# A change to the feed-forward half of a decoder layer: plain products for one column set of down, earlier residual loads, token sums split by adding transfers, gelu and splits at a later place on ScalarE

## The chip, the cores and the metric

The kernel runs on one core of a Trainium2 chip. The metric is the device time of one execution in microseconds (us). Engines are named as in the profile: PE is TensorE's matmul, PEld its weight load, DVE is VectorE, ACT is ScalarE, POOL is GpSimd, SP is SyncE, which does nothing here but issue DMAs.

## The reference

A decoder layer for 512 tokens of width 2048 in float32: four attention groups, an output projection, a layer norm, a gated feed-forward part, a second layer norm. The change touches the feed-forward part alone.

```python
D_MODEL, SEQ, D_FF, CONV_WIDTH = 2048, 512, 5632, 3

def conv_ffn(x, w_up, conv_w, conv_b, w_down):
    S = x.shape[1]
    u, g = jnp.split(x @ w_up, 2, axis=-1)
    gp = jnp.pad(g, ((0, 0), (CONV_WIDTH - 1, 0), (0, 0)))
    gc = conv_b
    for tap in range(CONV_WIDTH):
        gc = gc + conv_w[tap] * gp[:, tap:tap + S]
    return (jax.nn.gelu(gc) * u) @ w_down
...
        h = layer_norm(DEEPNORM_ALPHA * h + mix, ln1_g[l], ln1_b[l])
        ffn = conv_ffn(h, ffn_w_up[l], ffn_conv_w[l], ffn_conv_b[l], ffn_w_down[l])
        h = layer_norm(DEEPNORM_ALPHA * h + ffn, ln2_g[l], ln2_b[l])
```

## The kernel before

**Numbers.** A float32 operand is held as a high and a low part in a shorter float format (fp32r); a product is three matmuls (`PARTS`: high-high, high-low, low-high). `split_pair` (L898) makes the parts: ACT copies the raw value into the high part (L899), DVE subtracts that from the raw value into the low part (L900).

**Units.** Both large products of the feed-forward part run in units of 84 matmuls of 128x256. A unit is a Strassen-Winograd step: 2x2 blocks, 7 block products (`UP`) for 8, of 12 matmuls each. Its operands are seven weight blocks (three of the blocks as they are, four sums) and seven token blocks (likewise). The part "up" is units 0 to 87: 44 columns of tiles `f`, two units each. The part "down" is units 88 to 129: `CHUNKS` cuts the hidden rows into three chunks of six row pairs `kp` and one of four; within a chunk the column sets `q` (four; three in the last chunk) run one after the other, each of three units of two `kp` (two units in the last chunk). So unit 88 is the first of down, unit 91 the first of its second column set, and units 100, 112 and 124 are the first of chunks 1, 2 and 3. The last quarter of the columns of the last chunk is done plainly at the end (the tail).

**Weights.** `next_unit` (L902) hands out a unit and at that place has the operands of the following one made by `weight_operands` (L909): SP loads two raw tiles `wr` of 512 KB (four buffers, two units); ACT writes the negative of three blocks into `wl` (L925); a DMA in POOL's queue adds the raw blocks to that in place (L926, 768 KB, so `wl` becomes raw minus its rounded value); ACT copies the blocks into `wh` (L928); POOL makes four sums `S` (L934 to L937), which `split_pair` splits into four `ws` pairs. `wh` and `wl` have two buffers each, `ws` six pairs, `S` two tiles. The first two units (f = 0) use plain products and fewer operands.

**Up's end.** After the second unit of an `f`, `up_finish` (L989) adds up the banks, and `gated` (L1003) makes the gate: ACT `c` (L1010), two DVE steps (L1011, L1013), gelu on ACT (L1015), the product with `up` on POOL (L1016). For every second `f`, `set_aside` makes four token sums `ht` on POOL (L1031 to L1036) and SP writes blocks and sums to HBM (`hid`).

**Hidden operands.** `hidden_operands(kp)` (L1071) has SP load the blocks (`hx`) and the sums (`hx` for a chunk's first two `kp`, `hxt` for the others) and splits them by `split_pair`. It is called for kp 0 to 3 in the first unit of the last `f`, for 4 and 5 at unit 88, and for the next chunk's six in the last column set of a chunk, two after each of its units.

**Down's end of a set.** In the last unit of a set, `down_add` (L1117) adds the seven banks to the accumulators `acc`; in chunk 0 the residual rows are loaded into these at that same unit (L1200).

**Order.** Code is written in the order of use; a scheduler places each instruction on its engine's list by a priority that goes with that order, moved by `high_priority` (weights 900 places ahead, hidden splits 10 ahead in chunk 0, 150 behind later). An engine runs its list in order; a DMA starts from the list of the engine that issues it, so a transfer of POOL's queue waits for all that stands before it on POOL.

## Time and profile before

| | us |
|---|---|
| runs | 2329.66, 2337.31, 2339.68 (median 2337.31) |
| profiled execution | 2341.35 |
| its span | 2339.6 |
| PE busy in the span | 2232.7 (95%) |
| DVE, POOL, ACT busy | 1591.7, 1368.4, 1229.5 |
| software DMA queue (POOL's), share of 16 engines | 102.24 MB, 24.6% |
| hardware DMA queue q1 (SP's) | 287.72 MB, 35.6% |

The span is the profiled execution from its first instruction to its last; 1.75 us of that execution lie outside of it. "Busy" is a sum over the span. PEclk is the granted clock of TensorE as a share of full speed (2.4 GHz; the other level is 1.2 GHz). Up runs from about 920 us to 1829.44, down from there to about 2281, the tail and the last layer norm to the end.

### The profile page before, as it was taken

The page shows a single profiled execution, that of the slowest core. Times are in us where ns is not written, and L with a number is a line of the kernel's source. Part 1 is how long each engine was busy: PE and PEld are TensorE (multiplying, and loading weights), DVE is VectorE, ACT ScalarE, POOL GpSimd, SP SyncE. Part 2 cuts the span into 40 slices and gives each one's busy share as a digit, 9 for nine tenths or more (in the row PEclk, how much of TensorE's full clock was granted, in tenths as well). Part 3 has the DMA queues.
Part 4 walks back from the last instruction along what each step waited for, and adds up shares of the span by engine and source line. Part 5 has one row for each costly group of instructions (what it writes and reads, how often), then busy time and mean ns, then how long its engine had stood idle before and what let it go on. Part 6 is the DMA issues. An engine that isn't in the chain of part 4 may idle for free. (4 is left out here: it accounts for less than half of the span.)

```text
span 2339.6 us, 40306 instructions
## 1 busy us (share of the span) xinstructions
PE 2232.7 (95%) x15454; PEld 2083.5 (89%) x15454; DVE 1591.7 (68%) x2204; ACT 1229.5 (53%) x2129; POOL 1368.4 (58%) x1197
## 2 busy tenths in 40 slices
PE   7999999999999998899999999999999899999995
PEld 6788888888888878899999999999999899899994
DVE  7544455456675348687787767777676878677778
ACT  5444453355563135565555555565555666565651
POOL 5212110123234517787887878877777687777874
PEclk9999999999999999999999999999999999999998
DMA  6322223222124363888888777777778888788873
GB/s 228 92 81 73 78 67 106 84 64 62 59 88 149 104 188 94 224 226 227 231 222 238 202 210 207 201 204 197 212 202 227 243 241 233 193 229 216 207 191 115
DMA packets 125362, 392.75 MB, mean 168 GB/s; under 512 B 13632, under 2 KB 23744, under 8 KB 125168
## 3 DMA queue, kind: packets, MB, share of 16 engines
q1 hardware_dynamic: 106304, 287.72, 35.6%
q0 software_dynamic: 18720, 102.24, 24.6%
q8 instruction: 121, 1.98, 0.3%
q14 instruction: 73, 0.60, 0.1%
q10 hardware_dynamic: 144, 0.21, 0.0%
HBM read 354.36 MB, written 35.65 MB: 167 GB/s over the span
## 5 line engine op out<-in xcount | busy, mean ns | idle before, releaser
L900 DVE TENSOR_TENSOR ws<-S,ws 128x512 fp32r<-128x512 f32 x512 | 600.1, 1192 | 244.3 <-ACT ws L899 238.9
L963 PE MATMUL up<-xt,ws 128*128 128x256 f32 x3096 | 386.4, 283 | 0.3 <-DVE ws L900 0.3
L963 PEld LDWEIGHTS up<-xt,ws 128*128 128x128 f32 x3096 | 378.0, 192 | 0.6 <-DVE ws L900 0.6
L899 ACT CAST ws<-S 128x512 fp32r<-128x512 f32 x512 | 307.0, 615 | 114.9 <-POOL S L934 33.5
L100 DVE TENSOR_TENSOR wl<-wr,wh 128x1024 fp32r<-128x1024 f32 x122 | 155.2, 1272 | 213.3 <-ACT wh L99 198.4
L936 POOL TENSOR_TENSOR S<-wr 128x512 f32<-128x512 f32 x128 | 212.0, 1656 | 92.5 <-DVE ws L900 87.3
L342 POOL TENSOR_SCALAR P<-P,r 128x128 f32<-128x128 f32 (+3 forms) x144 | 81.1, 582 | 308.5 <-DVE r L337 166.2
L963 PE MATMUL up<-x,wh 128*128 128x256 f32 x1376 | 258.8, 288 | 0.0
L99 ACT CAST wh<-wr 128x1024 fp32r<-128x1024 f32 x122 | 128.0, 1049 | 233.7 <-PE op L733 78.8
L934 POOL TENSOR_TENSOR S<-wr 128x512 f32<-128x512 f32 x128 | 183.8, 1436 | 108.0 <-issue 45.3
L925 ACT ACTIVATE wl<-wr 128x512 fp32r<-128x512 f32 (+1 forms) x260 | 205.1, 836 | 67.3 <-PE dn L1115 43.5
L928 ACT CAST wh<-wr 128x512 fp32r<-128x512 f32 (+1 forms) x260 | 211.5, 829 | 35.7 <-PE up L963 33.8
L963 PE MATMUL up<-x,wl 128*128 128x256 f32 x688 | 200.8, 292 | 29.5 <-DMA wl<-in_wup_dram 29.3
L963 PEld LDWEIGHTS up<-x,wh 128*128 128x128 f32 x1376 | 220.5, 197 | 0.0
L937 POOL TENSOR_TENSOR S<-wr,S 128x512 f32<-128x512 f32 x128 | 211.8, 1655 | 0.0
L935 POOL TENSOR_TENSOR S<-S,wr 128x512 f32<-128x512 f32 x128 | 198.5, 1551 | 9.7
L1115 PE MATMUL dn<-wh,hx 128*128 128x256 f32 x792 | 157.5, 292 | 13.3 <-DVE acc L1128 8.6
L963 PEld LDWEIGHTS up<-x,wl 128*128 128x128 f32 x688 | 135.8, 197 | 33.7 <-DMA wl<-in_wup_dram 33.7
L1115 PEld LDWEIGHTS dn<-wh,hx 128*128 128x128 f32 x792 | 132.3, 200 | 14.9 <-issue 6.3
L733 PE MATMUL op<-wh,oTs 128*128 128x512 f32 x448 | 140.6, 391 | 0.0
L963 PE MATMUL up<-x,ws 128*128 128x256 f32 x1032 | 137.9, 283 | 0.0
L1015 ACT ACTIVATE c<-c 128x512 f32<-128x512 f32 x44 | 27.8, 632 | 208.0 <-DVE c L1013 208.0
(327 smaller groups left out, 5321.3 us busy)
## 6 DMA issues: line engine op xcount, KB each, us to landing
wr<-in_wup_dram SPq DMA_DIRECT2D x176, 512.0 KB
wl<-in_wup_dram POOLq DMA_DIRECT2D x88, 768.0 KB, 7.5
wr<-in_wm_dram SPq DMA_DIRECT2D x84, 512.0 KB
wr<-in_wdown_dram SPq DMA_DIRECT2D x84, 512.0 KB
wl<-in_wdown_dram POOLq DMA_DIRECT2D x42, 768.0 KB, 7.4
wr<-in_wout_dram SPq DMA_DIRECT2D x32, 512.0 KB
hid<-c SPq DMA_DIRECT2D x44, 256.0 KB
hid<-ht SPq DMA_DIRECT2D x44, 256.0 KB
```

What stands on the lines that cost most here:

```text
L100: nc.vector.tensor_sub(l[:, :cols], raw[:, :cols], h[:, :cols].bitcast(F32))
L733: nc.tensor.matmul(ps, ot[ct][:, a, t * P:(t + 1) * P], w[b][:, c2 * 512:(c2 + 1) * 512], start=(first and (a, b) == (0, 0)), stop=(last a ...
L899: self.nc.scalar.copy(h, raw)
L900: self.nc.vector.tensor_sub(l, raw, h.bitcast(F32))
L925: nc.scalar.mul(l3[:, o], i, -1.0)
L928: nc.scalar.copy(h3[:, o], i)
L934: nc.gpsimd.tensor_add(s12[:, 0], a21, a22)
L935: nc.gpsimd.tensor_sub(s12[:, 1], s12[:, 0], a11)
L936: nc.gpsimd.tensor_sub(s34[:, 0], a11, a21)
L937: nc.gpsimd.tensor_sub(s34[:, 1], a12, s12[:, 1])
L963: self.nc.tensor.matmul(ps, w[iw][i][:, k * P:(k + 1) * P], x[j][ix], start=(opens and k == 0 and (i, j) == (0, 0)), stop=(last and k == 3 ...
L1115: self.nc.tensor.matmul(bk[i][:, a * 256:(a + 1) * 256], x[ix][j][:, a * P:(a + 1) * P], w[iw][p][:, q * 256:(q + 1) * 256], start=first a ...
```

## The change

Four edits, all in the feed-forward part.

1. The first column set of chunk 0 (units 88 to 90) is made of plain products: 48 matmuls of 256 columns and 24 of 512 per unit, on four banks. These units need no weight sums; the low parts of their weights come from DVE (`split_pair`), and not from the adding DMA.
2. In chunk 0 the residual rows are loaded at the first unit of a set and not at its last.
3. `hidden_added`: for the last four `kp` of each chunk (two in the last one), 14 of 22, the low part of the token sums `hxt` is made as that of the weights is: ACT writes the negative, a DMA in POOL's queue adds the 512 KB from HBM, ACT copies the high part in place. These are ACT and POOL instructions of 1024 columns, for two ACT and two DVE instructions of 512 before.
4. `deferred` and `run_deferred`: gelu with what follows it, and all splits of hidden operands, are put behind `mark`, the last ACT copy of the following unit's weights.

The new `plain_products` and `plain_add` are in the diff; the removed body of `hidden_operands` is the one printed above.

```diff
@@ -896,14 +896,24 @@
     def split_pair(self, raw, h, l):
-        self.nc.scalar.copy(h, raw)
+        ins = self.nc.scalar.copy(h, raw)
         self.nc.vector.tensor_sub(l, raw, h.bitcast(F32))
+        return ins
+    def run_deferred(self):
+        with self.tc.issue_after(self.mark.ins):
+            while self.deferred:
+                self.deferred.popleft()()
     def next_unit(self):
         w = self.unit
+        self.w12 = self.w12_next
         self.unit = self.weight_operands(self.units.popleft()) if self.units else None
         self.unit_no += 1
+        self.run_deferred()
         return w
     def weight_operands(self, src):
@@ -913,6 +923,8 @@
         nc = self.nc
         with self.tc.high_priority(offset=900 if self.unit_no > 1 else 200):
+            plain = self.unit_no < 2 or 2 * FT <= self.unit_no < 2 * FT + 3
             raw = [self.pW.tile([P, 2, 512], F32, tag="wr", name="wr", bufs=4) for _ in range(2)]
             for p in range(2):
                 nc.sync.dma_start(raw[p], src[:, 2 * p:2 * p + 2])
@@ -921,14 +933,20 @@
             a22 = raw[1][:, 1]
             h3, l3 = (self.pW.tile([P, 3, 512], F32R, tag=g, name=g, bufs=2)
                       for g in ("wh", "wl"))
-            for o, i in ((slice(0, 1), raw[0][:, 1:2]), (slice(1, 3), raw[1])):
-                nc.scalar.mul(l3[:, o], i, -1.0)
-            nc.gpsimd.dma_start(l3, src[:, 1:4], accum_op=ALU.add)
-            for o, i in ((slice(0, 1), raw[0][:, 1:2]), (slice(1, 3), raw[1])):
-                nc.scalar.copy(h3[:, o], i)
-            if self.unit_no < 2:
+            blocks = ((slice(0, 1), raw[0][:, 1:2]), (slice(1, 3), raw[1]))
+            if self.unit_no < 2 * FT or not plain:
+                for o, i in blocks:
+                    nc.scalar.mul(l3[:, o], i, -1.0)
+                nc.gpsimd.dma_start(l3, src[:, 1:4], accum_op=ALU.add)
+                for o, i in blocks:
+                    nc.scalar.copy(h3[:, o], i)
+            else:
+                for o, i in blocks:
+                    self.split_pair(i, h3[:, o], l3[:, o])
+            if plain:
                 w = [self.tmp("w21", dt=F32R, tag="w") for _ in range(2)]
-                self.split_pair(a21, *w)
+                self.mark = self.split_pair(a21, *w)
+                self.w12_next = h3[:, 1:3], l3[:, 1:3]
                 return [[h3[:, i], l3[:, i]] for i in range(3)] + [w]
             s12, s34 = (self.pP.tile([P, 2, 512], F32, tag="P", name="S") for _ in range(2))
             nc.gpsimd.tensor_add(s12[:, 0], a21, a22)
@@ -939,7 +957,7 @@
             for t in (s12, s34):
                 for i in range(2):
                     ws.append([self.tmp("ws", dt=F32R, tag="w") for _ in range(2)])
-                    self.split_pair(t[:, i], *ws[-1])
+                    self.mark = self.split_pair(t[:, i], *ws[-1])
         return [[h3[:, i], l3[:, i]] for i in range(3)] + ws
@@ -981,7 +999,7 @@
         self.step_aside()
         if (f, n) == (FT - 1, 0):
             for kp in range(4):
-                self.hidden_operands(kp)
+                self.hidden_blocks(kp)
         if n == 1:
             self.up_finish(f, self.bk.pop(f)[0])
@@ -1012,6 +1030,10 @@
                                        op1=ALU.add)
         nc.vector.scalar_tensor_tensor(c[:, 2:], g[:, :510], cw(0), c[:, 2:], op0=ALU.mult,
                                        op1=ALU.add)
+        self.deferred.append(lambda: self.activate(f, c, up))
+    def activate(self, f, c, up):
+        nc = self.nc
         nc.scalar.activation(c, c, AF.Gelu_apprx_tanh)
         (nc.vector if f == 0 else nc.gpsimd).tensor_mul(c, c, up)
         c = c.rearrange("p (a n) -> p a n", a=2)
@@ -1068,45 +1090,96 @@
     SLOTS = 6
-    def hidden_operands(self, kp):
...
+    def hidden_split(self, srcs, tiles):
+        for (h, l), src in zip(tiles, srcs):
             with self.tc.high_priority(offset=10):
...
+                self.nc.sync.dma_start(l.bitcast(F32), src)
+        def split():
+            for h, l in tiles:
+                self.split_pair(l.bitcast(F32), h, l)
+        self.deferred.append(split)
+    def hidden_added(self, src, h, l):
+        nc = self.nc
+        with self.tc.high_priority(offset=10):
+            nc.sync.dma_start(h.bitcast(F32), src)
+        def split():
+            nc.scalar.mul(l, h.bitcast(F32), -1.0)
+            nc.gpsimd.dma_start(l, src, accum_op=ALU.add)
+            nc.scalar.copy(h, h.bitcast(F32))
+        self.deferred.append(split)
+    def hidden_blocks(self, kp):
+        def pair(n):
             if n == 2:
...
+                return [self.tmp("hx", (P, 2, 256), F32R) for _ in range(2)]
+            o = self.tmp("hx", (P, 2, 1, 256), F32R)
+            return o[:, 0], o[:, 1]
+        sizes = (2, 1, 1) if kp < self.SLOTS else (2, 2) if kp >= 18 else (2, 1)
+        tiles = [pair(n) for n in sizes]
+        ops, srcs = [], []
+        for t, n in zip(tiles, sizes):
+            srcs.append(self.hid[kp][:, len(ops):len(ops) + n])
+            ops += [[h[:, k] for h in t] for k in range(n)]
+        self.hidden_split(srcs, tiles)
+        self.ho[kp] = ops
+    def hidden_sums(self, kp):
+        if kp % self.SLOTS >= 2:
+            whole = [self.pT.tile([P, 4, 256], F32R, tag="T", name="hxt") for _ in range(2)]
+            xt = [[x[:, i:i + 2] for x in whole] for i in (0, 2)]
         else:
             xt = [[self.tmp("hx", (P, 2, 256), F32R) for _ in range(2)] for _ in range(2)]
...
+        if kp % self.SLOTS >= 2:
+            self.hidden_added(self.hid[kp][:, 4:8], *whole)
+        else:
+            self.hidden_split([self.hid[kp][:, i:i + 2] for i in (4, 6)], xt)
+        ops = self.ho[kp]
+        self.ho[kp] = (ops[:3] + [[h[:, k] for h in x] for x in xt for k in range(2)] + ops[3:])
+    def plain_products(self, bk, w, u):
+        for k in range(2):
+            ops = self.ho[2 * u + k]
+            cols = slice(k * 256, (k + 1) * 256)
+            for t in range(NT):
+                a = slice(t % 2 * P, t % 2 * P + P)
+                for j, p in self.PARTS:
+                    first = u == 0 and k == 0 and (j, p) == (0, 0)
+                    x1, x2 = (ops[i][j][:, a] for i in ((0, 1), (-1, 2))[t // 2])
+                    for n, iw in enumerate((0, 3)):
+                        self.nc.tensor.matmul(bk[t][:, n * 256:(n + 1) * 256], x1,
+                                              w[iw][p][:, cols], start=first and n == 0,
+                                              stop=False, skip_group_check=True)
+                    self.nc.tensor.matmul(bk[t].rearrange("p (a n) -> p a n", a=2), x2,
+                                          self.w12[p][:, :, cols], start=False,
+                                          stop=u == 2 and k == 1 and (j, p) == (1, 0),
+                                          skip_group_check=True)
+    def plain_add(self, acc, bk):
+        nc = self.nc
+        for t in range(NT):
+            o = acc[t // 2][:, t % 2]
+            if t < 2:
+                nc.vector.tensor_add(o, o, bk[t])
+            else:
+                nc.vector.tensor_add(o[:, :256], o[:, :256], bk[t][:, :256])
+                nc.scalar.copy(o[:, 256:], bk[t][:, 256:])
+        c22 = acc[1][:, :, 256:]
+        for o in (acc[0][:, :, 256:], acc[1][:, :, :256]):
+            nc.gpsimd.tensor_sub(o, o, c22)
     def down_product(self, bk, w, i, q, x, first, last):
         _, _, iw, ix = self.UP[i]
@@ -1181,25 +1254,39 @@
             if n and 2 <= f < 18:
                 self.up_residual(f - 2)
         self.st2 = [self.cst.tile([P, 4, 6], F32, name=f"st2_{t}") for t in range(NT)]
-        self.due = deque((4, 5))
+        self.due = deque()
         acc = []
         token = lambda t, q: acc[q][t // 2][:, t % 2]
         for c, k0, nk in self.CHUNKS:
             sets = self.column_sets(c)
             for q in sets:
-                bk = [self.bank("g" if i < 3 else "a", "dn") for i in range(7)]
+                plain = (c, q) == (0, 0)
+                bk = [self.bank("g" if i < 3 else "a", "dn") for i in range(4 if plain else 7)]
                 nu = nk // 2
                 for u in range(nu):
                     w = self.next_unit()
                     self.step_aside()
-                    if c == 0 and u == nu - 1:
+                    if c == 0 and u == 0:
                         acc.append([self.pT.tile([P, 2, 512], F32, tag="T", name="acc")
                                     for _ in range(2)])
                         for t in range(NT):
                             cols = 512 if t < 2 else 256
                             nc.sync.dma_start(token(t, q)[:, :cols], self.res[t][q][:, :cols])
                     while self.due:
-                        self.hidden_operands(self.due.popleft())
+                        kp = self.due.popleft()
+                        self.hidden_blocks(kp)
+                        self.hidden_sums(kp)
+                    if plain:
+                        if u == 0:
+                            for kp in (4, 5):
+                                self.hidden_blocks(kp)
+                        for kp in (2 * u, 2 * u + 1):
+                            self.hidden_sums(kp)
+                        self.plain_products(bk, w, u)
+                        if u == nu - 1:
+                            self.plain_add(acc[q], bk)
+                        continue
                     for i in range(7):
                         for k in range(2):
                             self.down_product(bk, w, i, k, self.ho[k0 + 2 * u + k],
```

Where instructions stand. The first place is ACT in up, before: `c_13278` is the gate of f = 18, `wh_13410` and `wl_13411` are weights of unit 40 (f = 20), the `ws` are the weight sums of unit 39.

```order
L1010 ACTIVATE c_13278<-g_13268,prm_83 128x512
L1015 ACTIVATE c_13278<-c_13278 128x512
L928 CAST wh_13410<-wr_13406 128x512
L925 ACTIVATE wl_13411<-wr_13406 128x512
L925 ACTIVATE wl_13411<-wr_13407 128x1024
L899 CAST ws_13313<-S_13300 128x512
L928 CAST wh_13410<-wr_13407 128x1024
L899 CAST ws_13317<-S_13300 128x512
```

After, the same instructions:

```order
L1028 ACTIVATE c_13278<-g_13268,prm_83 128x512
L942 CAST wh_13410<-wr_13406 128x512
L939 ACTIVATE wl_13411<-wr_13406 128x512
L939 ACTIVATE wl_13411<-wr_13407 128x1024
L899 CAST ws_13311<-S_13298 128x512
L942 CAST wh_13410<-wr_13407 128x1024
L899 CAST ws_13315<-S_13298 128x512
L1037 ACTIVATE c_13278<-c_13278 128x512
```

Gelu stands six places later, behind the weights; so it does for 40 of the 44 `f`. POOL in up, before (`c_14056` is the gate of f = 21, `wl_14194` a weight of unit 46):

```order
L935 TENSOR_TENSOR S_14200<-S_14200,wr_14189 128x512
L1016 TENSOR_TENSOR c_14056<-c_14056,up_14053 128x512
L1032 TENSOR_TENSOR ht_14184<-c_14056,ht_14184 128x256
L1035 TENSOR_TENSOR ht_14185<-c_14056,c_13799 128x256
L1036 TENSOR_TENSOR ht_14185<-c_14056,ht_14184 128x256
L926 DMA wl_14194<-in_wup_dram 128x1536
```

And after:

```order
L953 TENSOR_TENSOR S_14200<-S_14200,wr_14189 128x512
L940 DMA wl_14194<-in_wup_dram 128x1536
L1038 TENSOR_TENSOR c_14056<-c_14056,up_14053 128x512
L954 TENSOR_TENSOR S_14201<-wr_14189 128x512
L955 TENSOR_TENSOR S_14201<-wr_14190,S_14200 128x512
L1054 TENSOR_TENSOR ht_14184<-c_14056,ht_14184 128x256
```

The DMA that makes `wl` is issued ahead of the product that needs gelu, and no longer behind it and three token sums.

The second place is ACT at the start of chunk 1. Before, `hxt_21371` are token sums of kp 8, `ws_21201` and `ws_21344` weight sums of units 99 and 100, and `wl_21510` belongs to unit 101.

```order
L899 CAST ws_21201<-S_21184 128x512
L899 CAST hx_21383<-hx_21384 128x512
L899 CAST ws_21344<-S_21338 128x512
L899 CAST hx_21386<-hx_21386 128x256
L899 CAST ws_21348<-S_21338 128x512
L899 CAST hxt_21371<-hxt_21372 128x512 x2
L1138 COPY acc_21361<-dn_21048 128x2x256
L925 ACTIVATE wl_21510<-wr_21505 128x512
```

After, `hxt_21286` and `hxt_21285` are the low and the high part of kp 8's sums, `ws_21430` is the last weight sum of unit 101, and `wh_21552` and `ws_21565` belong to unit 102.

```order
L899 CAST ws_21430<-S_21413 128x512
L942 CAST wh_21552<-wr_21549 128x1024
L899 CAST ws_21565<-S_21559 128x512
L899 CAST hx_21280<-hx_21281 128x512
L899 CAST ws_21569<-S_21559 128x512
L899 CAST hx_21282<-hx_21282 128x256
L1113 ACTIVATE hxt_21286<-hxt_21285 128x1024
L899 CAST hx_21288<-hx_21289 128x512
L1115 CAST hxt_21285<-hxt_21285 128x1024
L899 CAST hx_21290<-hx_21290 128x256
L1113 ACTIVATE hxt_21294<-hxt_21293 128x1024
L1115 CAST hxt_21293<-hxt_21293 128x1024
```

The splits of kp 8 and 9, which unit 101 uses, stood ahead of unit 101's weights and now stand behind them and behind two weight sums of unit 102.

The third place is POOL at the handover from up to down, before (`wl_20038` is a weight of one of down's first units):

```order
L934 TENSOR_TENSOR S_20044<-wr_20033,wr_20034 128x512
L1016 TENSOR_TENSOR c_19724<-c_19724,up_19721 128x512
L935 TENSOR_TENSOR S_20044<-S_20044,wr_20033 128x512
L1031 TENSOR_TENSOR ht_19910<-c_19724 128x256
L926 DMA wl_20038<-in_wdown_dram 128x1536
```

After (`wl_20078` is the weight of unit 91, the first with seven products, and the two `hxt` belong to kp 2 and 3):

```order
L1114 DMA hxt_19996<-hid2_9931 128x1024
L952 TENSOR_TENSOR S_20217<-wr_20206,wr_20207 128x512
L954 TENSOR_TENSOR S_20218<-wr_20206 128x512
L953 TENSOR_TENSOR S_20217<-S_20217,wr_20206 128x512
L1114 DMA hxt_19999<-hid3_10468 128x1024
L955 TENSOR_TENSOR S_20218<-wr_20207,S_20217 128x512
L940 DMA wl_20078<-in_wdown_dram 128x1536
```

Unit 91's transfer stands behind two adding transfers of token sums and behind the weight sums of unit 92.

## Rows read from the trace of the kernel before

**Rows 1.** The page: busy time by engine, share of the span, instructions.

```profile
PE 2232.7 (95%) x15454; PEld 2083.5 (89%) x15454; DVE 1591.7 (68%) x2204; ACT 1229.5 (53%) x2129; POOL 1368.4 (58%) x1197
```

**Rows 2.** PE's waits in up (840 to 1800 us): total, times, longest.

```profile
PE up L963 <- DMA wl<-in_wup_dram: 24.8, 19, 5.6
```

**Rows 3.** Stretches of the span: length, busy time of the engines, clock.

```profile
core 0: us, PE busy (x) PEld busy (x) DVE busy (x) ACT busy (x) POOL busy (x), PEclk, DMA share, GB/s
1008.50:1803.10 794.60, 775.48 (x6387) 771.83 (x6386) 594.99 (x634) 455.98 (x719) 632.04 (x493) 0.99 0.81 214
...
1984.90:2015.90 31.00, 23.78 (x171) 23.11 (x170) 18.83 (x24) 16.51 (x27) 24.78 (x18) 0.83 0.74 193
```

**Rows 4.** PE's timeline: pitch of 256 columns in up, of 512 in the projection.

```profile
1297.34 1.60 PE L963 MATMUL up<-x,ws 128*128 128x256 f32 x12
1298.78 0.40 PE L963 MATMUL up<-x,wh 128*128 128x256 f32 x2
...
799.23 0.61 PE L733 MATMUL op<-wh,oTs 128*128 128x512 f32 x2
...
801.95 0.39 PE L733 MATMUL op<-wh,oTs 128*128 128x512 f32 x1
```

**Rows 5.** PE's timeline in up, unit 18: start, microseconds, in brackets the wait.

```profile
1091.37 0.40 PE L963 MATMUL up<-x,wh 128*128 128x256 f32 x2
...
1096.27 0.58 PE L963 MATMUL up<-x,wl 128*128 128x256 f32 x1 [4.51 <-DMA wl<-in_wup_dram]
```

**Rows 6.** POOL's timeline ahead of that wait.

```profile
1079.67 1.62 POOL L935 TENSOR_TENSOR S<-S,wr 128x512 f32<-128x512 f32 x1
...
1082.64 1.30 POOL L1016 TENSOR_TENSOR c<-c,up 128x512 f32<-128x512 f32 x1 [0.20 <-ACT c L1015]
...
1087.05 0.87 POOL L926 DMA_DIRECT2D wl<-in_wup_dram  x1
```

**Rows 7.** ACT's timeline at the same place.

```profile
1081.93 0.63 ACT L1015 ACTIVATE c<-c 128x512 f32<-128x512 f32 x1 [5.98 <-DVE c L1013]
...
1082.98 1.58 ACT L925 ACTIVATE wl<-wr 128x512 fp32r<-128x512 f32 x2
```

**Rows 8.** Groups by line and form: busy, mean ns, idle before.

```profile
L1015 ACT ACTIVATE c<-c 128x512 f32<-128x512 f32 x44 | 27.8, 632 | 208.0 <-DVE c L1013 208.0
L900 DVE TENSOR_TENSOR hxt<-hxt 128x512 fp32r<-128x512 f32 x28 | 26.1, 950 | 3.5 <-ACT hxt L899 3.4
L925 ACT ACTIVATE wl<-wr 128x1024 fp32r<-128x1024 f32 x130 | 135.7, 1044 | 0.0
L934 POOL TENSOR_TENSOR S<-wr 128x512 f32<-128x512 f32 x128 | 183.8, 1436 | 108.0 <-issue 45.3 <-DVE ws L900 31.9 <-POOL S L937 11.7
```

**Rows 9.** PE's timeline: starts of units 86, 87 and 94, and unit 86's wait.

```profile
1803.08 0.40 PE L963 MATMUL up<-x,wh 128*128 128x256 f32 x2
...
1807.98 0.58 PE L963 MATMUL up<-x,wl 128*128 128x256 f32 x1 [4.50 <-DMA wl<-in_wup_dram]
...
1819.37 0.40 PE L963 MATMUL up<-x,wh 128*128 128x256 f32 x2
...
1904.04 0.28 PE L1115 MATMUL dn<-wh,hx 128*128 128x256 f32 x1
```

**Rows 10.** PE's timeline: starts of units 102, 104, 114 and 116.

```profile
1984.88 0.28 PE L1115 MATMUL dn<-wh,hx 128*128 128x256 f32 x1
...
2015.89 0.28 PE L1115 MATMUL dn<-wh,hx 128*128 128x256 f32 x1
...
2116.69 0.28 PE L1115 MATMUL dn<-wh,hx 128*128 128x256 f32 x1
...
2143.83 0.28 PE L1115 MATMUL dn<-wh,hx 128*128 128x256 f32 x1
```

**Rows 11.** All adding transfers of L926, issue to landing; and the issue of unit 86's.

```profile
DMA to landing us min/median/max: 6.5/7.5/11.7
...
1796.81 0.87 POOL L926 DMA_DIRECT2D wl<-in_wup_dram  x1
```

More of the change, by code (lines that the diff above doesn't have):

```diff
@@ L63, in __init__ @@
         self.every, self.count = 24, 0
-        self.late = deque()
+        self.late, self.deferred = deque(), deque()
         self.ahead = 0
-        self.unit, self.unit_no = None, 0
+        self.unit, self.unit_no, self.w12_next = None, 0, None
     def tmp(self, name, shape=(P, 512), dt=F32, tag="t"):
@@ L1069 @@
     SLOTS = 6
-    def hidden_operands(self, kp):
-        nc = self.nc
-        j = kp % self.SLOTS
-        ops = []
-        loaded = []
-        ahead = 10 if kp < self.SLOTS else -150
-        def load(h, l, src):
-            with self.tc.high_priority(offset=10):
-                nc.sync.dma_start(l.bitcast(F32), src)
-            loaded.append((l.bitcast(F32), h, l))
-        for i, n in ((0, 2), (2, 2 if kp >= 18 else 1)):
-            if n == 2:
-                o = [self.tmp("hx", (P, 2, 256), F32R) for _ in range(2)]
-            else:
-                o = self.tmp("hx", (P, 2, 1, 256), F32R)
-                o = o[:, 0], o[:, 1]
-            load(*o, self.hid[kp][:, i:i + n])
-            ops += [[h[:, k] for h in o] for k in range(n)]
-        b12 = ops[3:]
-        ops = ops[:3]
-        if j >= 2:
-            xt = [self.pT.tile([P, 4, 256], F32R, tag="T", name="hxt") for _ in range(2)]
-            xt = [[x[:, i:i + 2] for x in xt] for i in (0, 2)]
+    def hidden_split(self, srcs, tiles):
[6 more added lines that the diff above has]
+        self.deferred.append(split)
@@ L1101, in hidden_operands @@
+    def hidden_sums(self, kp):
+        if kp % self.SLOTS >= 2:
+            whole = [self.pT.tile([P, 4, 256], F32R, tag="T", name="hxt") for _ in range(2)]
+            xt = [[x[:, i:i + 2] for x in whole] for i in (0, 2)]
         else:
             xt = [[self.tmp("hx", (P, 2, 256), F32R) for _ in range(2)] for _ in range(2)]
-        for i in range(2):
-            load(*xt[i], self.hid[kp][:, 4 + 2 * i:6 + 2 * i])
-            ops += [[h[:, k] for h in xt[i]] for k in range(2)]
-        with self.tc.high_priority(offset=ahead):
-            for raw, h, l in loaded:
-                self.split_pair(raw, h, l)
@@ L1109, in hidden_operands @@
-        self.ho[kp] = ops + b12
+        if kp % self.SLOTS >= 2:
[21 more added lines that the diff above has]
+                                          skip_group_check=True)
```

1 line of the change is left out of this document (added).

## The prediction

> **What bounds the kernel now.** I read the page's busy times first, then PE's waits by stage, then the starts of PE's units, and then what ACT and POOL did ahead of the waits. PE is busy for 2232.7 us of the span, 95%, and no other engine is above 68% [rows 1]: the kernel is bound by PE, and only what shortens PE's own work or its waits can move the end. A unit without a wait takes 84 matmuls of 256 columns; 12 of them follow one another in 1298.78 − 1297.34 = 1.44 us [rows 4], so 0.12 us each and 10.08 us for a unit. What a stretch takes beyond 10.08 us for each of its units I call its excess.
>
> There are three stretches with excess that the change touches.
>
> *Up*, from unit 10 to the end of unit 85: 794.60 us [rows 3] for 76 units, which are 766.1 us. Excess 28.5 us. One wait makes nearly all of it: PE waited 24.8 us, in 19 places, for the low parts `wl` of up's weights [rows 2].
>
> *The handover*, units 86 to 93: 1904.04 − 1803.08 = 100.96 us [rows 9] for 80.64. Excess 20.3 us. Unit 86 shows a price that I need below: its wait of 4.50 us made the unit 16.29 us long, 6.2 too long [rows 9]. A waited microsecond costs some 1.4, since the clock falls with the wait: over such a stretch the mean grant was 0.83 of 2.4 GHz, between the levels of 1.2 and 2.4 [rows 3].
>
> *The chunks of down*: units 102 and 103 took 2015.89 − 1984.88 = 31.01 us, units 114 and 115 took 27.14 [rows 10], each for 20.16. Excess 10.85 and 6.98, together 17.8 us.
>
> **The change part by part.**
>
> *Gelu later.* In unit 17 POOL finished the sum of line 935 at 1081.29 us. On its list a token sum, the product with gelu and three more token sums stood next, and the transfer that makes `wl` was issued at 1087.05 [rows 6], 5.8 us later. Unit 18 began at 1091.37 and stood still for 4.51 us until 1096.27 [rows 5]. ACT held it too: it sat idle for 5.98 us ahead of gelu, which waited for the second DVE step of the gate, and the negatives that the transfer adds to came behind gelu and ended at 1084.56 [rows 7]. This repeats: gelu has 208.0 us of idle time ahead of it over 44 instructions, all of it for that DVE step [rows 8]. After the change the weights stand ahead of gelu on ACT, and the transfer ahead of the product on POOL. An issue at 1081.3 with the median 7.5 us to landing [rows 11] ends at 1088.8, ahead of the unit. So this wait goes, and with it the half clock behind it. Added is a wait: POOL's product now waits for a gelu that stands behind the next unit's last `ws` copy. Queued behind it on POOL are two weight sums and the token sums; ACT's later `ws` copies wait for those. They are a unit ahead of their use, and POOL is busy for only 632 of the 794.6 us [rows 3], so I cost this at nothing; if the cover fails, the wait moves from `wl` to `ws` and the gain is gone (rival D). I take −25 us: the excess of 28.5 less some 3.5 for transfers that are late for other reasons. Bounds: −28.5, and −12 if half of the 19 waits stay.
>
> *The plain set.* A unit then has 48 matmuls of 0.12 us and 24 of 512 columns. For these the projection gives the pitch: 12 of them from 799.23 to 801.95 us, 0.227 each [rows 4]. 5.76 + 5.44 = 11.20 us, 1.12 more than now, +3.4 for three. In return these units need no weight sums (four of 1.44 us or more on POOL, the row of L934 in [rows 8], with four ACT copies and four DVE subtractions each), and no adding transfer; the residual loads at a set's first unit fall into this slack and cost nothing, as SP's queue has room there. So the 14 us of excess from unit 87 on should mostly go, and unit 86's 6.2 too, since its transfer is no longer held by gelu. What is late next is unit 91, the first with seven products. There are two buffers of `wl`, and a plain unit uses its own up to its end; unit 91's buffer is free when unit 89 ends. From there two negatives (1.04 us for the longer) [rows 8], then POOL, where the transfer stands behind two adding transfers of token sums, then 7.5 us: about 13 to 16 us, against the 11.2 of unit 90. I take a wait of 4.5 us at a price of 1.4, 6.5, and 1 for unit 88. New excess 3.4 + 6.5 + 1 = 10.9 for 20.3: −9.5. Bounds −14 (unit 91 waits for 1.5 us) and −5.
>
> *Splits behind the weights, sums by adding transfers.* DVE is freed of 28 subtractions, 26.1 us in all [rows 8]; DVE was not the bound, so that is worth nothing by itself. What counts is when the token sums are ready. Now kp 8's sums are copied on ACT ahead of unit 101's weights. After the change they stand behind unit 101's last weight sum and two of unit 102's, and the sixth pair of `ws` is free only as PE leaves unit 100. So the negative of kp 8 comes about 2.5 us into unit 101, and the transfer's issue, behind a sum on POOL, at 3.5. No row shows an adding transfer of 512 KB; the nearest ones are those of 768 KB, at 6.5, 7.5 and 11.7 us (least, median, most) [rows 11]. I take the median, since the DMA engines are as loaded there. Then the sums are there at 11.0 us; PE, which takes products with blocks first, wants them at about 6.3. Wait 4.7, cost 6.6 us. Unit 102 first waits some 3 us for ACT, which is behind, and then some 3.5 for the fourth transfer: 9.1. Unit 100 loses 1.5 to blocks that are split late. That makes 17.2 for each of two boundaries, and 9.1 at the third, where a chunk has one such unit: 43.5 instead of 17.8, +25.7. The Trainium skill, page "DMA: Bandwidth & Descriptors", section "Anatomy of one DMA — SWDGE (gpsimd) path", gives 2.0 us and the bytes at 436 GB/s for one transfer. By it 512 KB would land in an estimated 3.2 us and 768 KB in 3.8; the trace has 6.5 at the least for the latter, so the trace disagrees with the rule for this kind of transfer under this load; by the rule the boundaries would lose nothing on token sums and the time would be about that of rival B.
>
> *Sum.* −25 − 9.5 + 25.7 = −8.8. The profiled execution took 2341.35 us, 4.04 more than the median of the runs, so 2332.5 for it and 2328.5 as a median: 2329.
>
> **The rivals.**
>
> *B, faster: the token sums come in time.* If time goes with bytes, 512 KB take 4.3 to 5.0 us (two thirds of 6.5 and 7.5). For it speaks that a boundary's transfers are few; against it that each follows another in POOL's queue. Unit 101 then waits 1.5 (2.1 us), unit 102 waits 3 for ACT (4.2), unit 100 loses 1.5: 7.8 twice and 4.2 make 19.8 instead of 17.8. −25 − 9.5 + 2 = −32.5, time about 2305.
>
> *C, slower: the adding transfers crowd one another.* Unit 86's transfer was issued at 1796.81 and PE went on at 1807.98 [rows 9, 11], 11 us later, where SP's loads of hidden rows ran beside it; a boundary of chunks is such a place as well. With 11 us for each, unit 101 waits 8.2 (11.5 us), unit 102 10 (14): 27 twice and 14 make 68, +50; the handover gains only 5. −25 − 5 + 50 = +20, about 2358. Each microsecond of transfer costs 1.4 in five units, 7 us; so from 8.8 us on the change is no gain, and it is slower by over 0.5% from about 10.4.
>
> *D, the change doesn't do what it says in up:* gelu moves, but POOL now waits for it at the product, the sums behind it come late, and PE waits as long for `ws` as it did for `wl`. POOL's 80% in that stretch [rows 3] speaks for it; against it speaks that of the 5.8 us between sum and issue POOL waited for gelu for 0.20 alone [rows 6]; the rest is work, which now stands behind the transfer. 0 − 9.5 + 25.7 = +16, about 2354.
>
> **How the numbers follow.** Forecast 0.53, B 0.25, C 0.12, D 0.10. A measurement of this kernel can tell 0.5%, 11.7 us, from no change: faster is below 2325.6, slower above 2349. The forecast's own bounds (up −12 to −28.5, handover −5 to −14, boundaries ±8) put about 0.15 of its chance below 2325.6, 0.36 between, 0.02 above. B is faster; of C 0.11 is slower, of D 0.06. Faster 0.40, same 0.41, slower 0.19. The range goes from B's time to D's, 2306 to 2354; the far half of B, and C, lie outside.
>
> **What would show it.** Right: from 1000 us on no wait for `wl` in up, and 76 units in about 770 us; the idle time ahead of gelu gone from ACT; units 88 to 90 of 11.2 us; a wait for `wl` in unit 91; waits for `hxt` in the second and third unit of chunks 1 and 2 and the second of chunk 3, with a lower granted clock there. Wrong: waits for `ws` in up, adding transfers of 512 KB well below 6 us (B), or at 9 and more (C). What the sum rests on most is the landing time of these transfers and the place of the splits behind the weights.

## The result and the profile after

The changed kernel takes 2402.22 us (median of 2399.19 to 2407.99) where the kernel before took 2336.56 beside it (2329.66 to 2339.68): 1.029 times as long, 95% interval 1.026 to 1.032. The forecast was 2329 us, with a range of 2306 to 2354: a small gain was expected, and the kernel is 2.9% slower. The profiled execution took 2400.65 us, with a span of 2398.6, 59.0 more than before.

The page of the changed kernel, first the busy times [rows 1], then the granted clock in 40 slices:

```profile
span 2398.6 us, 40151 instructions
...
PE 2250.6 (94%) x15418; PEld 2094.4 (87%) x15418; DVE 1531.4 (64%) x2176; ACT 1241.2 (52%) x2119; POOL 1355.5 (57%) x1196
...
PEclk9999999999999999999999999999999898989988
```

PE's busy time rose by 18 us and the span by 59: what was added is waiting, and in five slices from 1859 us on, most of them in down, the granted clock is below nine tenths of 2.4 GHz. DVE and POOL have less to do than before, as the change meant, and it does not show in the time.

Where the 59 us are is read from the starts of PE's units, as ahead of the prediction. All executions below are profiled ones. The least is 10.08 us for each unit, 11.20 for each of the three plain ones.

| stretch (units) | least | before | after | difference | forecast |
|---|---|---|---|---|---|
| 10 to 41 | 322.6 | 342.0 | 348.1 | +6.1 | |
| 42 to 85 | 443.5 | 452.6 | 443.5 | −9.1 | −25, both rows |
| 86 to 93 | 80.6 | 101.0 | 100.9 | 0.0 | −9.5 |
| 94 to 99 | 60.5 | 60.7 | 60.5 | −0.2 | 0 |
| 100 to 111 (chunk 1) | 121.0 | 131.8 | 154.3 | +22.5 | |
| 112 to 123 (chunk 2) | 121.0 | 127.9 | 154.2 | +26.2 | |
| 124 to the end | | 115.1 | 128.1 | +13.0 | +25.7, three rows |

With 0.5 us ahead of unit 10 the differences make 59.0. Each kernel is read from one execution, and these differ: from unit 100 on the kernel before took 374.9 us in its own, and seven kernels below that have its code in down took 362.3 to 367.8 in theirs. So a difference of some 10 us there is not safe; one of 60 is.

PE's waits after, as before in total, times and longest: first units 10 to 41 (between 1005 and 1360 us), then from 1940 us to the end. For units 42 to 85 the view is empty.

```profile
PE up L981 <- DMA wl<-in_wup_dram: 16.3, 11, 2.1
PE up L981 <- DVE ws L900: 4.4, 3, 3.0
```

```profile
PE dn L1188 <- DMA hxt<-hid: 25.1, 6, 7.8
PE dn L1188 <- DVE hx L900: 22.0, 19, 2.3
PE dn L1188 <- ACT ws L899: 5.3, 2, 2.7
PE dn L1188 <- DVE acc L1201: 3.5, 1, 3.5
```

In the second view two waits are new: for the adding transfers of the token sums (25.1 us), and for hidden blocks that DVE has not split yet (22.0 us). Before, PE waited for 16.1 us in all from 1940 us on, for accumulators, weights and once for a weight sum.

The stretches 10 to 41, 42 to 85 and chunk 1, after and then before, with columns as in [rows 3]:

```profile
1008.98:1357.08 348.10, 327.42 (x2691) 324.58 (x2689) 270.58 (x287) 196.01 (x304) 270.36 (x211) 1.00 0.84 221
1357.08:1800.60 443.52, 443.52 (x3699) 443.52 (x3698) 307.13 (x350) 269.26 (x417) 369.70 (x289) 1.00 0.84 210
1962.00:2116.30 154.30, 132.87 (x1010) 130.62 (x1009) 92.41 (x97) 81.71 (x129) 99.04 (x73) 0.90 0.76 193
```

```profile
1008.50:1350.50 342.00, 329.66 (x2691) 327.83 (x2689) 264.63 (x284) 194.42 (x304) 272.44 (x211) 0.98 0.84 226
1350.50:1803.08 452.58, 445.80 (x3699) 443.97 (x3697) 330.34 (x351) 261.54 (x415) 359.59 (x283) 1.00 0.78 204
1964.72:2096.53 131.81, 124.59 (x1010) 123.92 (x1009) 94.49 (x105) 78.17 (x129) 99.46 (x69) 0.96 0.80 208
```

In units 42 to 85 PE is busy for all of the 443.52 us: gelu's later place has taken away every wait there (the run of gelu alone, below, shows that it is gelu's place). In units 10 to 41 it has not. In chunk 1 POOL, ACT and DVE are busy for less than two thirds of the stretch and the DMA share fell from 0.80 to 0.76: nothing there is at its limit, it is a chain of waits, and the mean clock over it is 0.90 of 2.4 GHz where it was 0.96.

### The profile page after: what moved, and what is told of

It reads as the page before. It is cut to its first block, busy times and chain, and to the rows that moved or that the text cites. A ratio compares the mean times of both kernels' runs of the same rounds, so it can differ in the third digit from the quotient of the medians.

```text
span 2398.6 us, 40151 instructions
## 1 busy us (share of the span) xinstructions
PE 2250.6 (94%) x15418; PEld 2094.4 (87%) x15418; DVE 1531.4 (64%) x2176; ACT 1241.2 (52%) x2119; POOL 1355.5 (57%) x1196
## 3 DMA queue, kind: packets, MB, share of 16 engines
q0 software_dynamic: 20304, 107.23, 25.1%
## 5 line engine op out<-in xcount | busy, mean ns | idle before, releaser
L900 DVE TENSOR_TENSOR ws<-S,ws 128x512 fp32r<-128x512 f32 x500 | 562.3, 1138 | 346.4 <-ACT ws L899 339.7
L939 ACT ACTIVATE wl<-wr 128x512 fp32r<-128x512 f32 x254 | 201.2, 837 | 182.9 <-PE dn L1188 151.5
L942 ACT CAST wh<-wr 128x512 fp32r<-128x512 f32 x254 | 207.1, 830 | 123.7 <-PE up L981 122.2
L954 POOL TENSOR_TENSOR S<-wr 128x512 f32<-128x512 f32 x125 | 195.8, 1567 | 111.3 <-DVE ws L900 110.3
L981 PE MATMUL up<-x,wh 128*128 128x256 f32 x1376 | 253.7, 284 | 0.0
L99 ACT CAST wh<-wr 128x1024 fp32r<-128x1024 f32 x122 | 128.0, 1049 | 239.6 <-PE op L733 78.7
L952 POOL TENSOR_TENSOR S<-wr 128x512 f32<-128x512 f32 x125 | 174.7, 1398 | 101.9 <-DMA wr<-in_wdown_dram 35.6
L953 POOL TENSOR_TENSOR S<-S,wr 128x512 f32<-128x512 f32 x125 | 192.7, 1542 | 9.0
L1188 PEld LDWEIGHTS dn<-wh,hx 128*128 128x128 f32 x736 | 127.3, 207 | 27.4 <-DVE hx L900 22.3
L1188 PE MATMUL dn<-ws,hx 128*128 128x256 f32 x972 | 134.5, 291 | 8.6 <-ACT ws L899 5.3
```

The costliest lines, as they stand in the source:

```text
L900: self.nc.vector.tensor_sub(l, raw, h.bitcast(F32))
L939: nc.scalar.mul(l3[:, o], i, -1.0)
L942: nc.scalar.copy(h3[:, o], i)
L952: nc.gpsimd.tensor_add(s12[:, 0], a21, a22)
L953: nc.gpsimd.tensor_sub(s12[:, 1], s12[:, 0], a11)
L954: nc.gpsimd.tensor_sub(s34[:, 0], a11, a21)
```

## The experiments

Two questions were put. In up: does gelu hold the transfers (the prediction's theory), or, theory R, does something else hold DVE in units 10 to 41, where the residual rows are scaled (`up_residual`, 16 of the 44 f)? In down: is it the adding transfer (theory T) or the place of the splits behind the weights (theory P)?

**Gelu alone.**

```diff
         nc.vector.scalar_tensor_tensor(c[:, 2:], g[:, :510], cw(0), c[:, 2:], op0=ALU.mult,
                                        op1=ALU.add)
+        self.deferred.append(lambda: self.activate(f, c, up))
```

(with `mark`, `run_deferred` and `activate` as in the change; the rest is the kernel before)

> The kernel before with one edit: gelu and what follows it stand behind the next unit's weights. Theory of the prediction (gelu holds the transfers of wl): the 28 us of excess of units 10 to 85 nearly all go, and unit 86's 6: about 2305 us. Theory R (in the first part of up it is the load of the residual rows that holds DVE, and gelu only in the second): units 10 to 41 keep some 19 to 25 us of excess, units 42 to 85 lose their 9, unit 86 its 6: about 2320 to 2328 us. Down as before under both.

Measured: 1.001 times the kernel before, 0.999 to 1.004. Units 42 to 85 took 443.5 us, all 9 us gained. Units 10 to 41 took 350.0, 8 us longer than before. Units 86 to 91 took 88.2 for 78.7. So gelu was the holder in the second part of up and not the one that counted in the first, and what it gave there was lost on both sides. The total that R named, 2320 to 2328, was missed (the median was 2342), since it counted no loss.

**Splits in place, sums by DVE, and both.** Three runs from the changed kernel: with the first edit below (sums by DVE), with the second, made in `hidden_split` and in `hidden_added` (splits in place), and with both.

```diff
-        if kp % self.SLOTS >= 2:
-            self.hidden_added(self.hid[kp][:, 4:8], *whole)
-        else:
-            self.hidden_split([self.hid[kp][:, i:i + 2] for i in (4, 6)], xt)
+        self.hidden_split([self.hid[kp][:, i:i + 2] for i in (4, 6)], xt)
...
-        self.deferred.append(split)
+        with self.tc.high_priority(offset=10 if kp < self.SLOTS else -150):
+            split()
```

> The changed kernel, but the token sums' low parts come from DVE (copy and subtraction) as before; all splits still stand behind the weights. Theory T (the adding transfers of 512 KB, 9 to 13 us from issue to landing, cost the 62 us from unit 100 on): most of it goes, some 45 to 50 us, about 2350 us. Theory P (the place of the splits behind the weights costs it, whoever makes the low parts): at most 15 us go, about 2390 us.

> The changed kernel with its adding transfers, but the hidden splits are not put behind the weights; they have the priority that they had in the kernel before. Theory T: the transfers take as long and PE waits for them: at least 40 of the 62 us stay, about 2380 us. Theory P: most goes, about 2350 us.

> The changed kernel with neither: token sums' low parts by DVE and hidden splits at their old priority. Left are the plain column set, the early residual loads and the later gelu. T and P: from unit 100 on as before (within 5 us), so 2330 to 2345 us; if it stays above 2370, neither is the cause.

The ratios are of all executions of each kernel, the units' times (us) of its profiled one.

| kernel | ratio to before (95%) | 88 to 91 | chunk 1 | chunk 2 | 124 to the end |
|---|---|---|---|---|---|
| before | | 52.3 | 131.8 | 127.9 | 115.1 |
| changed (late, adding) | 1.029 (1.026 to 1.032) | 59.9 | 154.3 | 154.2 | 128.1 |
| late, DVE | 1.011 (1.009 to 1.013) | 59.2 | 139.2 | 139.5 | 126.5 |
| in place, adding | 1.010 (1.007 to 1.012) | 72.4 | 126.9 | 127.7 | 119.0 |
| in place, DVE | 1.005 (1.004 to 1.007) | 65.4 | 126.2 | 131.7 | 117.1 |

Neither theory holds alone. From unit 100 on the changed kernel takes 61.7 us more than before. With the place alone (late, DVE) it is 30.3, with the adding transfers alone (in place, adding) −1.2, with neither 0.1. So from unit 100 on the adding transfers cost nothing where they are issued early, the late place costs 30 us by itself, and on top of the late place the transfers cost 31 more. At the handover the transfers cost something in place as well: units 86 to 93 took 121.6 us with them and 109.4 without, and the medians of the two kernels, 2361.7 and 2348.4 us, are 13 apart. T expected at least 40 us to stay with the splits in place; P expected at most 15 us to go with sums by DVE, and 31 went. None of the totals named for the three runs was met: the medians were 2365.8, 2361.7 and 2348.4 us.

The adding transfers were not much faster in place than late. From issue to landing, least, median and most, of the changed kernel and then of the one with the splits in place:

```profile
DMA to landing us min/median/max: 5.4/10.0/12.9
```

```profile
DMA to landing us min/median/max: 6.1/8.5/9.7
```

What differs most is when they are issued. In the changed kernel, in unit 101, first ACT's and POOL's rows of kp 8, then PE's in units 101 and 102:

```profile
1981.11 1.05 ACT L1113 ACTIVATE hxt<-hxt 128x1024 fp32r<-128x1024 f32 x1
```

```profile
1984.41 0.89 POOL L1114 DMA_DIRECT2D hxt<-hid  x1
```

```profile
1995.07 0.79 PE L1188 MATMUL dn<-wh,hxt 128*128 128x256 f32 x2 [7.35 <-DMA hxt<-hid]
...
2005.21 0.39 PE L1188 MATMUL dn<-ws,hx 128*128 128x256 f32 x1 [2.67 <-ACT ws L899]
...
2018.59 0.80 PE L1188 MATMUL dn<-wh,hxt 128*128 128x256 f32 x2 [3.46 <-DMA hxt<-hid]
```

Issued at 1984.41, landed 10.6 us later, and PE stood for 7.35 us. While PE stands, unit 101 keeps its weight buffers, ACT cannot begin the next weights (it sat idle for 14.60 us until 2000.56 for that), and so unit 102 waits for weight sums (2.67) and again for a transfer (3.46). The kernel with the splits in place waits for 5.4 us in all for these transfers, in 4 places.

The handover, units 88 to 91, goes the other way: it is worst with the splits in place.

**The plain set with the early residual loads** (the run with both edits above, and gelu where it was):

```diff
-        self.deferred.append(lambda: self.activate(f, c, up))
+        self.activate(f, c, up)
```

> The changed kernel with the splits in place, token sums by DVE, and gelu where it was: what is left is the plain column set with the early residual loads. As forecast (9.5 us gained from unit 86 to 91): about 2328 us. If the plain set itself brings the 7 us that units 86 to 91 took longer in the run that had also gelu later: about 2345 us; if gelu's delay of the last hidden rows brings it: about 2337 us.

Measured: 1.007 (1.005 to 1.009), 2355 us, above all three numbers. Units 86 to 91 took 91.2 us, 12.6 more than before; the forecast had 9.5 less. PE waited in unit 91 for the plain set's banks to be added up on DVE:

```profile
1880.22 0.55 PE L1187 MATMUL dn<-wh,hx 128*128 128x256 f32 x1 [13.69 <-DVE acc L1175]
```

The banks were added up late because the two additions stood on DVE behind a split of hidden blocks, whose load SP issued only at 1870.01:

```profile
1877.80 0.92 ACT L899 CAST hx<-hx 128x512 fp32r<-128x512 f32 x2 [11.54 <-DMA hx<-hid]
```

```profile
1878.45 1.03 DVE L900 TENSOR_TENSOR hx<-hx 128x512 fp32r<-128x512 f32 x2 [11.61 <-ACT hx L899]
1879.40 1.28 DVE L1175 TENSOR_TENSOR acc<-acc,dn 128x512 f32<-128x512 f32 x2
```

Ahead of that load SP stood for 9.3 us for a token sum of POOL, and POOL had stood for 13.64 us for raw weights, whose loads SP issued at 1852.84, behind five residual rows and a wait for DVE to free their buffers. With gelu late and the rest the same (in place, DVE) the banks cost 3.1 us of waiting, and PE waited 9.4 us for `wl` and 5.2 for the plain units' `wh`. So the plain set with the early residual loads is a loss, whether the splits stand in place or behind the weights (the wait for `wl` below). Which of these two edits makes it was not run.

**What holds DVE in units 10 to 41.** DVE's waits there, before and after:

```profile
DVE res L1054 <- DMA res<-res: 43.2, 13, 5.2
```

```profile
DVE res L1076 <- DMA res<-res: 56.3, 14, 9.6
```

One stall of the changed kernel, from engine to engine: SP's issue of the row, DVE's wait for it, POOL's wait for DVE, PE's wait for DVE.

```profile
1058.49 0.46 SPq L1075 DMA_DIRECT2D res<-res  x1
```

```profile
1070.84 0.69 DVE L1076 SCALAR_TENSOR_TENSOR res<-res,g 128x512 f32<-128x512 f32 x1 [9.62 <-DMA res<-res]
```

```profile
1073.41 1.66 POOL L954 TENSOR_TENSOR S<-wr 128x512 f32<-128x512 f32 x1 [10.10 <-DVE ws L900]
```

```profile
1072.19 2.50 PE L981 MATMUL up<-xt,ws 128*128 128x256 f32 x10 [3.00 <-DVE ws L900]
```

DVE stood for 9.62 us for one row, 12.35 us after its issue, with the subtractions for `ws` queued behind it. The runs that follow try to take this wait away. The first two put a row's two DVE steps one f behind its load in the code, with gelu later and without:

```diff
-        a = self.tmp("res")
+        a, gb = self.tmp("res"), self.gb1
         nc.sync.dma_start(a, self.res[t][n])
+        yield
         nc.vector.scalar_tensor_tensor(a, a, ALPHA, gb[0], op0=ALU.mult, op1=ALU.mult)
```

> The kernel before with gelu later (as in the run of that alone) and with each residual row of up loaded one f before DVE works on it. Theory R: the 27 us of excess that units 10 to 41 kept with gelu later alone go, these 32 units take about 325 us, not 350; the rest as with gelu later alone: about 2310 to 2316 us. Theory of the prediction (gelu): no further gain, about 2335 us.

> The kernel before with the earlier residual loads alone, gelu where it was. Theory R: units 10 to 41 lose most of their 19 us of excess, down to the rate of units 42 to 85 (some 6 us left for gelu); units 42 to 85 keep 9: about 2325 us. Theory of the prediction: no change, 2337 us.

Measured: 1.002 (1.000 to 1.004) and 1.000 (0.997 to 1.002); units 10 to 41 took 349.0 and 340.8 us. This says nothing on R: DVE waited for the rows as before, 56.4 us in 14 places in the first of them. The edit had moved nothing in the trace: by the code the steps of the row loaded at f = 4 come after the gate of f = 5, but its load was issued at 1014.26 and the first step began at 1021.64, still right behind the gate of f = 4 (before, 1012.84 and 1021.58). Both totals named under R were missed with it (the medians were 2342 and 2338 us).

A third run, made from the first of these, gives the last three f their old gelu, to see what made the handover longer in the run of gelu alone:

```diff
+        if f < FT - 3:
             self.deferred.append(lambda: self.activate(f, c, up))
+        else:
+            self.run_deferred()
+            self.activate(f, c, up)
```

> Gelu later and the earlier residual loads, but the last three f with gelu where it was, so that the last hidden rows are not written later. If the delay of these rows made units 86 to 91 some 9 us longer with gelu later, units 86 to 91 take 79 us again and the time is 2302 to 2308 us; if not, the same as the run without this exception.

Measured: 0.997 (0.995 to 0.999), units 86 to 91 in 72.1 us, not 88.2. So the late gelu of the last f's did delay the handover of this kernel, and the forecast lacked that. What it cost in the changed kernel is not shown: with the plain set, splits in place and sums by DVE, units 86 to 91 took 85.6 us with gelu late and 91.2 with gelu where it was. Units 10 to 41 still took 351.9, so the total (2330 us) missed the 2302 to 2308. To this kernel the next three edits were made. Rows in buffers of their own:

```diff
-        a, gb = self.tmp("res"), self.gb1
+        a, gb = self.cst.tile([P, 512], F32, tag="bias", name="res", bufs=2), self.gb1
```

> As the run with gelu later but for the last three f, and the residual rows in two buffers that are free all through up, so that their loads stand far ahead on SP (in the runs before, the loads could not move: their buffer came free late). The gains and offsets of a set of columns are still loaded late, four times. Theory R (DVE waits for the load of residual rows in units 10 to 41): stalls remain at the four places where gains are loaded, units 10 to 41 take some 335 us, not 352, and the whole some 15 us less than the run without these buffers, about 2315. Other theory (gelu or the rate of the transfers): 350 us again, no gain.

Measured: 1.001 (0.999 to 1.003), and units 10 to 41 took 354.5. The rows came early, but the gains came late, and the work of several rows then stood in one place: DVE waited 29.4 us in 3 places for rows and 7.3 for gains, and a single unit took 18.9 us. R's number was missed; the wait had been gathered, not removed. So the rows were left out:

```diff
-            if n and 2 <= f < 19:
-                if f > 2:
-                    next(ahead)
...
```

> The same kernel with the scaling of the residual rows in up left out (loads, two DVE steps and a store per f for 16 f), so the residual enters unscaled and this part of the work is missing. Theory R: units 10 to 41 take 323 to 326 us, as fast as units 42 to 85; about 2300 us. If they stay at 345 or more, the residual rows are not the cause of the stalls in up.

Measured: 2296.7 us, one execution; units 10 to 41 took 322.56 us, exactly 32 × 10.08. With gelu later, the residual rows are the cause of all excess there. Last, the work is kept and only its place on DVE is moved, by one f:

```diff
+        with self.tc.issue_after(self.gate.ins):
             nc.vector.scalar_tensor_tensor(a, a, ALPHA, gb[0], op0=ALU.mult, op1=ALU.mult)
             nc.vector.scalar_tensor_tensor(a, gb[1], ALPHA, a, op0=ALU.mult, op1=ALU.add)
```

(`gate` is the gate's last DVE step in the following f.)

> Gelu later but for the last three f, and the two DVE steps on a residual row put behind the gate's last DVE step of the following f, some 20 us after the row's load was issued; nothing left out. Theory R: DVE no longer waits for the rows, units 10 to 41 take 323 to 328 us as without the rows, and the whole 2298 to 2308 us, faster than the kernel before by over 1%. If the rows' own work on DVE and the DMA queue costs the time, and not the wait, units 10 to 41 stay at 340 or more.

Measured: 2301.86 us, 0.985 of the kernel before (0.983 to 0.987). Units 10 to 41 took 322.56 us. DVE's waits in that stretch, and PE's from 1005 to 1800 us:

```profile
DVE ws L900 <- ACT ws L899: 59.9, 23, 4.5
```

```profile
PE up L970 <- DMA wl<-in_wup_dram: 2.9, 1, 2.9
```

The wait for rows is gone, and so are both parts of up's excess, 28.5 us; one wait of 2.9 us is left, at the handover. (This execution is 39.5 us shorter than that of the kernel before. 11.0 of them lie from unit 100 on, where the code is the same and single executions differ by as much.) This kernel beats both; it takes of the change only the later gelu, but for the last three f.

**Is the transfer's time in its bytes?** From the kernel with the splits in place, adding transfers of half the size:

```diff
-            self.hidden_added(kp, self.hid[kp][:, 4:8], *whole)
+            self.hidden_added(kp, self.hid[kp][:, 4:6], *xt[0])
+            self.hidden_split(kp, [self.hid[kp][:, 6:8]], xt[1:])
```

> The changed kernel with the splits at their old place and adding transfers of 256 KB, for two of the four token sums; the other two by DVE. If the time of such a transfer goes with its bytes (8.2 to 9.0 us for 512 KB when the splits stand in place), 256 KB land in 4.1 to 4.5 us; if it goes with what else is on the DMA engines or is fixed per transfer, in 6.5 to 8.5 us.

```profile
DMA to landing us min/median/max: 4.4/7.0/9.2
```

Half the bytes took 7.0 us where the whole took 8.5 (median): the time does not go with the bytes. The 768 KB of the weights took 7.5 [rows 11], less than the 512 KB of the sums.

What the time does go with can be read from the issues and landings of the changed kernel. Of its 127 transfers of 768 KB, the 98 that had no other transfer of POOL's queue under way beside them took 6.9 us in the median (at most 10.7); the 6 that shared at least 4 us with another took 10.0 to 12.4. Of its 14 transfers of 512 KB, 13 shared that much: at a boundary they are issued in pairs, less than 2 us apart. At the start of chunk 1, first the two pairs (1980 to 2014 us), then the weights' four transfers between and behind them, each alone (2000 to 2045 us):

```profile
DMA to landing us min/median/max: 8.9/10.5/12.2
```

```profile
DMA to landing us min/median/max: 6.5/6.8/6.9
```

So it is rival C's reason, transfers that crowd one another, that fits; no run spaced the pairs out to test it.

## Why the prediction was wrong, step by step

*Gelu later, −25: wrong by 22.* The step that failed is "so this wait goes", taken from one stall and carried to all 19. Gelu was one holder of POOL's transfers; in units 10 to 41 there was a second one. There DVE stood for residual rows, 43.2 us in 13 places, with the subtractions for `ws` behind them on its list; POOL's weight sums waited for these, and the next transfer stood behind the sums on POOL's list. POOL's waits for `ws` in that stretch, before and after:

```profile
POOL S L936 <- DVE ws L900: 31.3, 16, 3.9
```

```profile
POOL S L954 <- DVE ws L900: 58.5, 14, 10.1
```

So the transfer is now issued ahead of gelu's product and PE waits all the same. The sign that the prediction took for "this repeats", gelu's 208.0 us of idle time [rows 8], does not tell the two stretches apart: before, it was 85.4 us ahead of 16 gelus in units 10 to 41 and 107.1 ahead of 22 in units 42 to 85. The row that named the second holder stood in [rows 8] as well, 31.9 us for `ws` ahead of the sum of L934, and was not priced. In units 42 to 85, without rows, the step was right to the last 0.1 us. Gelu's row after has 38.0 us of idle time ahead of it, none of it in units 42 to 85:

```profile
L1037 ACT ACTIVATE c<-c 128x512 f32<-128x512 f32 x44 | 27.7, 630 | 38.0 <-DVE c L1031 38.0
```

Of rival D the condition came true in small part: in units 10 to 41 PE's waits for `ws` are 4.4 us, and were nothing before, but those for `wl` are 16.3.

*The plain set, −9.5: wrong by 9.5.* The 11.20 us for a unit held: units 88 to 90 ran from 1820.76 to 1855.12, 34.36 us for 33.6. Unit 86's excess went too (86 and 87 took 20.16). What failed is the wait of unit 91, put at 4.5 us:

```profile
1868.12 0.58 PE L1188 MATMUL dn<-wl,hx 128*128 128x256 f32 x1 [12.72 <-DMA wl<-in_wdown_dram]
```

The transfer was issued at 1856.49, after unit 91 had begun, and took 11.6 us, not 7.5. From the end of unit 89 (1843.19) to the landing it took 24.9 us, where 13 to 16 were forecast. The prediction put the delay on the two adding transfers ahead of it on POOL; the run with sums by DVE has none of these and waits 12.67 us at the same place. What both runs have is that the negatives for unit 91 stand on ACT behind a weight sum of unit 92, which POOL makes only when unit 92's raw weights are there: in the changed kernel POOL began it at 1850.47 and ACT the negatives at 1852.32. With sums by DVE POOL stood 9.66 us for these raw weights, and the transfer landed 13.0 us after its issue.

*Splits and adding transfers, +25.7: right in sign, wrong by 36.* Units 100 to 103 took 73.7 us for 40.3 and units 112 to 115 73.6, an excess of 33 at each of these boundaries where 17.2 was put. Three terms were too small. A transfer was put at 7.5 us, from the weights' rows; measured are 10.0 late and 8.5 in place. The wait of unit 101 for the sums, put at 4.7, was 7.35, and unit 100, put at a cost of 1.5 for blocks that are split late, waited 2.01, 0.83 and 2.32. And the late place was priced mainly through the transfers, where by itself it makes 30.3 of the 61.7 us. Rival C had the transfer's time nearly right (11 us), and its reason; its +20 fell short of the 59.0 by the gain in up that did not come (22), by 12 at the boundaries and by 5 at the handover. Rival B, with 4.3 to 5.0 us for a transfer, is excluded: no run shows one of 512 KB under 5.4. By the rule of the Trainium skill, page "DMA: Bandwidth & Descriptors", section "Anatomy of one DMA — SWDGE (gpsimd) path", 512 KB would land in an estimated 3.2 us; the traces disagree.

*The early residual loads* were put at nothing, as SP's queue had room. They were not run by themselves, and no view shows PE waiting for them; but in the run with the plain set and gelu where it was, five of them stand on SP ahead of raw weights that came late, so this term is not shown to be nothing.

Open are: what an adding transfer of 512 KB takes when it flies alone; why units 10 to 41 became 6 us longer with gelu later, where DVE's wait for the rows rose from 43.2 to 56.3 us; what moving the rows' DVE steps is worth with gelu where it was; and what share of the 31 us that the transfers add to the late place is their own landing and what the weights that come late behind them.

## What to carry to other kernels

When an engine's idle time is put down to another engine, go on to that engine's own waits in the same stretch before pricing the edit, and do it for each stretch that differs in its work: here one view of DVE's waits, split at unit 42, would have told that DVE stood for residual rows where two thirds of up's excess lay. A price taken from one stall holds for others only where the same engines stand behind them. A step that waits for a DMA costs its engine's whole queue; putting it a fixed distance of work behind the load's issue, as was done with the rows, removed the wait at no cost that shows in these units, while distance in the code alone did nothing: in the trace the steps stood in their old place. Work may be put behind the next stage's only if it is not due in that next stage: gelu was not, but for the last three f; the hidden splits were.

## What the runs showed of the hardware that was not expected

An adding transfer's time hardly follows its size: 256 KB took 7.0 us in the median, 512 KB 8.5 (splits in place) and 10.0 (late), 768 KB 7.5. It goes with what else of POOL's queue is under way: 768 KB took 6.9 us in the median alone and 10.0 to 12.4 beside another for 4 us or more. A load of a residual row of 256 KB, issued behind two of 512 KB and two of gains, let DVE go on only 12.35 us after its issue; for the other 15 rows it was 6.4 to 9.5.
